# A hybrid decoder step on one core: branch 3's turned queries loaded two residues ahead, exchanged copies in a tile of their own, the weights of gb issued behind the attention, one buffer in another pool

## The chip, the cores and the metric

The kernel runs on one core of a Trainium2 chip. Its time is the device time of one execution in microseconds; the figure before the change is the median of three runs, 1337.58 us (1333.66 to 1339.45). Rows of the profile come from one further execution that was recorded by the hardware profiler.

## The reference

One inference step of a one-layer decoder with d = 1024, for a prompt of 2048 positions and a sample of 8 sequences with 8 new positions each. After an RMS norm one input projection gives the queries, keys and values (q, k, v) of mixer A, those of mixer B (qb, kb, vb), a low-rank gate input and two output gates:

```python
z = h @ w_in
q, k, v, qb, kb, vb, g_lr, gate_a, gate_b = jnp.split(z, split_points(), axis=-1)
q = rope(rmsnorm(heads(q, H_A), q_norm_w), pos)
k = rope(rmsnorm(heads(k, H_A), k_norm_w), pos)
o_a = attend(q, k, v)
log_a = jax.nn.log_sigmoid((g_lr @ w_gate_up + b_gate).astype(jnp.float32)) / GATE_TAU
o_b, s_fin = gla_chunked(heads(qb, H_B) * (DK_B ** -0.5), heads(kb, H_B), heads(vb, H_B),
                         heads(log_a, H_B), s0)
y = x + mixed.astype(x.dtype) @ w_out
```

Mixer A is a sliding-window attention with 8 heads of 64 in three branches of (window, dilation) = (128, 1), (512, 4), (2048, 16), mixed by their softmax denominators. In the third branch a position sees only positions of its own residue mod 16, so for the prompt it is 16 separate causal attentions of 128 rows each. Mixer B is a gated linear attention (GLA) with 4 heads. `mixed` is both mixers' outputs times their gates' SiLU.

## The kernel before, in words

Products are made of 16-bit halves (a value is split into a high and a low part), so one projected tile of 128 rows takes three matmuls for each of eight pieces of 128 input columns: `acc_vb` is 24 matmuls of 512 columns, `acc_g` is 24 of 272 and 24 of 256. TensorE is PE, VectorE DVE, ScalarE ACT, GpSimd POOL; SP issues all DMAs, in order.

The stages, by the trace: up to 500 us the projections q, k, v with branches 1 and 2 beside them; 500 to 623 us the projection qkb (the queries and keys of mixer B) beside the rest of the attention; 623 to 728 us branch 3; 728 to 985 us the projections g (gates) and vb with the GLA of the prompt; 985 to 1070 us the projection gb (the last gates) with the GLA of the sample; then the output projection, tile by tile, with the attention of the sample.

Branch 3 has a `branch3(r)` for each residue r (line 912), which gives two items `(r, 0)` and `(r, 1)` of four heads each to the queue `work`. A pipeline (line 1074) carries each item through three steps while the next ones follow: `qk` (scores `s` on PE at line 444, mask and maximum on DVE at 452, exponential `p` on ACT at 455), `tr` (PE turns the probabilities, `t` at 462, split into `pt` by ACT, DVE or POOL at 424 to 429) and `pv` (`O` at 477, its two parts added by ACT's `ol` at 493 and DVE's `o` at 494, stored by SP at 937). Ahead of the scores of a residue stands `pre` (line 915). It calls `turned3(r + 1)`, which lets SP load queries and keys of the next residue turned by the DMA (lines 906 to 910), and then `exchanged` (lines 815 to 818): two DVE copies of `T_q`, whose 128 partitions are two halves of 64, into the second half of the same tile with these halves swapped. Each score is a sum of two matmuls, one with the queries as loaded and one with the exchanged ones, against the keys `T_k`. `T_q` and `T_k` have two buffers each, so the load for residue r takes the buffer of r − 2 and waits for its last scores.

Beside the attention run the *host*, which deals out a projection's matmuls (`rest`, `project`), and `load_w`, which loads a projection's weights in eight pieces (line 601, tiles `wr_`), squares each on ACT for its size (line 622, `jw_`), works out a scale and splits each piece (lines 649 and 650). `weave` (line 358) mixes such parts by their share of steps done; `load_w("gb")` is a part of the second `weave` (line 1522). The sequence in which `weave` emits instructions is not the final one: a scheduler at compile time reorders each engine's program by a model of when data and buffers are ready. So a load of weights can move far ahead, as the weights of gb do: they are loaded in the middle of branch 3.

`qk_post` (line 684) makes the rotary form of q and k with two scratch tiles `t1` and `t2` from the pool `zp` (line 697); the pool `xp` closes with the projections q, k, v, before `b3`, the pool of branch 3, is opened in its place. `zp` stays open until the output stage's pools for the sample's attention take its place.

In the GLA, `gT_e`, `kq_e`, `la_e` are the first steps of a pair of chunks (e0 is the first): gate inputs and keys turned by PE and taken out by ACT, and the log of the gate in three ACT steps (lines 216 to 218); DVE scans it (223), ACT makes `eb_e` (227), then the `E` of each level (244), and PE the scores `sc_e` (281).

Of the kernel before, what the change touches and what calls it, by code (L numbers as in the profile page):

```python
# [7 lines left out]
F32 = mybir.dt.float32  # L8
F32R = mybir.dt.float32r
F16 = mybir.dt.float16  # L10
# [8 lines left out]
P = 128  # L19
# [33 lines left out]
def tile_hymba(ctx: ExitStack, tc: tile.TileContext, A: dict):  # L53
# [293 lines left out]
    def by16(ap, r):  # L347
        return ap.rearrange("(i r) c -> r i c", r=16)[r]
# [33 lines left out]
    with ExitStack() as c1:  # L382
# [206 lines left out]
        def load_w(name, between=(), behind=()):  # L589
# [7 lines left out]
            for k in range(KT):  # L597
                if k % 2 == 0:
                    pair = wr.tile([P, 2, 528], F32, name=f"wr_{name}_{k}", tag="wr")
                raw = pair[:, k % 2]  # L600
                SP.dma_start(raw[:, :n], src[k * P : (k + 1) * P, c0 : c0 + n])
                raws.append(raw)
                if k == KT // 2 - 1:
                    for f in between:
                        fetch(f)
# [78 lines left out]
        def qk_post(names, n, t):  # L684
# [9 lines left out]
                ct[:n, :, :g], cs[:n].unsqueeze(2).to_broadcast([n, 2, g, 64]),  # L694
                tabs[:n, :, i0 : i0 + g], ALU.mult,
            )
            t1 = zp.tile([P, 2, 512], F32, name=f"t1_{tag}", tag="z3", bufs=1)
            t2 = zp.tile([P, 2, 512], F32, name=f"t2_{tag}", tag="z4", bufs=1)
            z4 = zs[:n, :g].rearrange("p g (h two d) -> p g h two d", two=2, d=32)
            t24 = t2[:n, :g].rearrange("p g (h two d) -> p g h two d", two=2, d=32)  # L700
# [200 lines left out]
            return out  # L901


        T3 = [{} for _ in range(16)]

        def turned3(r):
            for nm_, src, nb in (("q", qp_d, 16), ("k", kp_d, 8)):
                t = b3.tile([P, nb, P], F16, name=f"T3_{nm_}_{r}", tag=f"T{nm_}")
                SP.dma_start_transpose(t[:, 0:8], by16(src, r))
                T3[r][nm_] = t  # L910

        def branch3(r):
            T = T3[r]

            def pre():
                if r == 0:
                    turned3(0)
                if r < 15:
                    turned3(r + 1)
                yield  # L920
                exchanged(
                    *(T["q"][:, a : a + 8].rearrange("p h i -> p (h i)") for a in (8, 0))
                )
                T["v"] = b3.tile([P, 1024], F16, name=f"v3_{r}", tag="v3")
                SP.dma_start(T["v"][:], by16(vp_d[:], r))
                for a in range(2):
                    T["o", a] = op.tile([P, 4, 66], F32, name=f"o3_{r}_{a}", tag="o")

            def OT(a, i):
                if ("O", a) not in T:  # L930
                    T["O", a] = ps_O.tile([P, 512], F32, name=f"O3_{r}_{a}", tag="O")
                return T["O", a][:, i * P : i * P + P]

            def post(a):
                o = T["o", a]
                added(o[:, :, 0:64], T["O", a][:])
                SP.dma_start(
                    by16(o3_d[:, 264 * a : 264 * a + 264], r), o[:].rearrange("p h d -> p (h d)")
                )

            return [
                attend(
                    f"3_{r}_{a}", 4, 1,
                    lambda i, a=a: [
                        (T["q"][:, 8 * part + 4 * a + i], T["k"][:, 4 * a + i])
                        for part in range(2)
                    ],
                    m3,
                    lambda i, b, a=a: T["v"][:, (4 * a + i) * P : (4 * a + i + 1) * P],
                    lambda i, a=a: T["o", a][:, i, 65:66],  # L950
                    lambda i, a=a: T["o", a][:, i, 64:65],
                    lambda i, a=a: OT(a, i),
                    pre=None if a else pre, post=lambda a=a: post(a), neg=scl["s"][:],
                )
                for a in range(2)
            ]
# [1073 lines left out]
```

## Time and profile before

| | |
|---|---|
| median of three runs | 1337.58 us |
| lowest and highest | 1333.66 and 1339.45 us |
| the profiled execution | 1341.12 us |
| its span in the profile | 1339.3 us |
| mean granted PE clock of it | 0.977 |

The profiled execution is 1.8 us longer than its span, and 1.7 us above the highest of the three. In the profile's rows, busy times are in microseconds of one engine, PEld is PE's loading of weights (beside PE's matmuls), and (x555) counts instructions. A row of waits has who waited, at which line, for what, then the total in us, how often, and the longest. A group of instructions has line, engine, operation, output and input by the program's names with buffer numbers left out, shape and count, then busy time and mean ns, then idle time ahead of them and what ended it. A row of the chain of waits has its start, its length and what it was; "issue" is time in which the engine waited for nothing that the profile shows. Rows of a timeline have start, length, engine (SPq is SP's queue of DMA issues), line and operation. A granted clock of 1.00 is PE's full speed.

### The profile page before, as it was taken

The page shows a single profiled execution, that of the slowest core. Times are in us where ns is not written, and L with a number is a line of the kernel's source. Part 1 is how long each engine was busy: PE and PEld are TensorE (multiplying, and loading weights), DVE is VectorE, ACT ScalarE, POOL GpSimd, SP SyncE. Part 2 cuts the span into 40 slices and gives each one's busy share as a digit, 9 for nine tenths or more (in the row PEclk, how much of TensorE's full clock was granted, in tenths as well). Part 3 has the DMA queues.
Part 4 walks back from the last instruction along what each step waited for, and adds up shares of the span by engine and source line. Part 5 has one row for each costly group of instructions (what it writes and reads, how often), then busy time and mean ns, then how long its engine had stood idle before and what let it go on. Part 6 is the DMA issues. An engine that isn't in the chain of part 4 may idle for free.

```text
span 1339.3 us, 26206 instructions
## 1 busy us (share of the span) xinstructions
PE 1215.7 (91%) x8878; PEld 726.8 (54%) x8878; DVE 924.8 (69%) x2275; ACT 876.6 (65%) x2332; POOL 635.4 (47%) x598
## 2 busy tenths in 40 slices
PE   3798999888899798998989899999999979999998
PEld 1343565555566555576667566676554434444443
DVE  6367767788677966776755988777682288778751
ACT  5655787777568875878986666666773366554630
POOL 0076554778678735661113975666362133232220
PEclk9998999999999999999999999999999989999999
DMA  8859856767966599969986556553236679998952
GB/s 256 248 159 254 234 174 155 208 204 216 222 180 192 174 265 281 317 208 212 214 186 184 171 179 200 163 156 119 88 126 192 193 229 342 358 380 293 320 191 79
DMA packets 251800, 285.27 MB, mean 213 GB/s; under 512 B 125441, under 2 KB 160338, under 8 KB 251666
## 3 DMA queue, kind: packets, MB, share of 16 engines
q1 hardware_dynamic: 251666, 283.60, 70.9%
q8 instruction: 70, 1.15, 0.4%
q14 instruction: 64, 0.52, 0.1%
HBM read 183.12 MB, written 75.24 MB: 193 GB/s over the span
## 4 chain that ended last, share of the span: by engine, by line
PE 38%; DVE 18%; DMA 16%; POOL 9%; issue 9%; ACT 8%; SPq 2%; POOLq 0%; DVEq 0%; ACTq 0%
PE Y L1652 4%; PE acc_qkb L1127 3%; PE acc_vb L1127 3%; PE acc_v L1127 3%; PE acc_g L1127 3%; PE acc_gb L1127 3%; PE O L477 3%; PE t L462 3%; PE s L444 3%; DVE qbd L252 3%; PE acc_q L1127 2%; DMA T_q<-qp_d 2%; POOL pr L965 2%; PE acc_k L1127 2%; DMA sv<-in_cache_v_win 2%
## 5 line engine op out<-in xcount | busy, mean ns | idle before, releaser
L1127 PEld LDWEIGHTS <-hr 128*128 128x128 f16 x1824 | 174.5, 99 | 134.3 <-issue 17.4
L1127 PEld LDWEIGHTS <-hl 128*128 128x128 f16 x1248 | 122.1, 100 | 151.8 <-issue 24.3
L455 ACT ACTIVATE p<-p,o 128x256 f32<-128x256 f32 (+1 forms) x384 | 173.3, 456 | 46.4 <-DVE o L452 39.4
L1652 PE MATMUL Y<-w_o,mh 128*128 128x512 f16 x768 | 176.7, 381 | 1.8 <-ACT mh L1611 1.8
L965 POOL TENSOR_TENSOR pr<-k,qb 128x512 f32<-128x512 f32 x96 | 132.5, 1381 | 91.2 <-DVE sck L970 57.1
L429 POOL TENSOR_TENSOR pt<-p,pt 128x512 f16<-128x512 f32 (+1 forms) x80 | 94.2, 1178 | 158.4 <-ACT pt L428 142.6
L477 PE MATMUL O<-v,pt 128*128 128x128 f16 x1200 | 111.4, 222 | 25.5 <-POOL pt L429 9.2
L1652 PEld LDWEIGHTS <-mh 128*128 128x128 f16 x768 | 72.0, 98 | 88.6 <-issue 6.3
L970 DVE TENSOR_REDUCE sck<-pr 128x8 f32<-128x512 f32 x128 | 85.6, 678 | 49.0 <-POOL pr L965 48.8
L462 PE MATMUL t<-ident,p 128*128 128x128 f32 x600 | 107.5, 284 | 8.1 <-ACT p L455 3.5
L1694 POOL TENSOR_TENSOR tc<-oc,w 128x512 f32<-128x512 f32 x32 | 45.2, 1432 | 141.9 <-DVE w L1686 119.1
L477 PEld LDWEIGHTS <-pt 128*128 128x128 f16 x1200 | 82.5, 99 | 51.2 <-POOL pt L429 14.1
L1127 PE MATMUL acc_v<-w_v,hl 128*128 128x512 f16 x384 | 96.4, 396 | 8.1 <-DMA hl<-early_ht 4.0
L1127 PE MATMUL acc_g<-w_g,hr 128*128 128x272 f16 (+1 forms) x768 | 102.6, 279 | 0.0
L452 DVE CUSTOM_DVE_ANT_0 p<-s,m3w,scl_s 128x128 f32<-128x128 f32 (+1 forms) x256 | 88.9, 394 | 11.6 <-PE s L444 6.2
L1127 PE MATMUL acc_q<-w_q,hl 128*128 128x512 f16 x384 | 91.6, 387 | 3.5 <-ACT zs_k L677 2.2
L244 ACT ACTIVATE E<-D_e 128x256 f32<-128x256 f32 x168 | 66.3, 417 | 43.5 <-POOL D_e L236 25.6
L1127 PE MATMUL acc_vb<-w_vb,hr 128*128 128x512 f16 x384 | 92.3, 389 | 2.4 <-ACT zg L733 2.4
L1127 PE MATMUL acc_k<-w_k,hl 128*128 128x512 f16 x384 | 89.9, 379 | 3.4 <-ACT zs_k L677 3.0
L444 PE MATMUL s<-kk,qq 128*128 128x256 f16 (+1 forms) x512 | 82.4, 272 | 9.7 <-DMA kk<-kp_d 6.1
L1127 PE MATMUL acc_gb<-w_gb,hr 128*128 128x512 f16 x384 | 87.1, 380 | 0.0
L462 PEld LDWEIGHTS t<-ident,p 128*128 128x128 f32 x600 | 69.4, 145 | 18.1 <-ACT p L455 8.1
(510 smaller groups left out, 2637.4 us busy)
## 6 DMA issues: line engine op xcount, KB each, us to landing
k<-in_cache_k_win SPq DMA_DIRECT2D x104, 256.0 KB
sv<-in_cache_v_win SPq DMA_DIRECT2D x24, 1024.0 KB
hr<-h_d SPq DMA_DIRECT2D x44, 512.0 KB
qb<-q_d SPq DMA_DIRECT2D x64, 256.0 KB
o_d<-o SPq DMA_DIRECT2D x96, 132.0 KB
oc<-o_d SPq DMA_DIRECT2D x48, 264.0 KB
x<-in_x_prompt SPq DMA_DIRECT2D x16, 512.0 KB
h_d<-hl SPq DMA_DIRECT2D x16, 512.0 KB
```

Source lines behind the costliest of these rows:

```text
L244: ACT.activation(ev[rows, i], dv[rows, :, half, :], AF.Exp, scale=(2 * half - 1) / 16.0)
L429: POOL.tensor_tensor(l, f, h, ALU.subtract)
L444: PE.matmul(s_ps[:, i * w : (i + 1) * w], q, k, start=(n == 0), stop=(n == len(prods) - 1),)
L452: DVE.tensor_tensor_reduce(s[:, sl], s_ps[:, sl], mask, neg, BIG, ALU.add, ALU.min, nmf(i))
L455: ACT.activation(s[:, sl], s[:, sl], AF.Exp, bias=nmf(i), scale=-1.0, accum_out=denf(i))
L462: PE.transpose(p_ps[:, i * P : (i + 1) * P], t["s"][:, i * P : (i + 1) * P], ident[:])
L477: PE.matmul(o_, t["pt"][:, c, (i * nb + b) * P : (i * nb + b + 1) * P], vf(i, b), start=(n == 0), stop=(n == 2 * nb - 1),)
L965: POOL.tensor_tensor(pr[:], kt, qt, ALU.mult)
L970: DVE.tensor_reduce(out, pr[:].rearrange("p (u k d) -> p u k d", u=2, k=4), AX.X, ALU.add)
L1127: PE.matmul(z, a_[:, k, :], w[:, p_, k, cols], start=(k == 0 and i == 0), stop=(k == KT - 1 and i == 2),)
L1652: PE.matmul(Y[:], a_[:, k, :], w_[:, part, k, :512], start=(i == 0), stop=(i == len(prods) - 1),)
L1694: eng.tensor_tensor(t_[:], oc[:, g, :, 0:64], w[:, g].unsqueeze(2).to_broadcast([P, NH, HD]), ALU.mult,)
```

## The change

Four edits:

- `turned3(r)` now loads the keys of residue r and the queries of r + 1, keys first; the queries have three buffers instead of two, so a query load takes the buffer of r − 3. One extra call, `turned3(-1)`, loads the queries of residue 0.
- The exchanged copies go to a tile `T_x` of their own; `T_q` holds 8 blocks instead of 16. The second product of each score reads `T_x`.
- The loads of the weights of gb, and only of gb, are tied by `tc.issue_after` to the last store of branch 3: SP issues them behind it.
- `t1` moves from the pool `zp` to the pool `xp`.

```diff
--- before.py
+++ after.py
@@ -598,7 +598,10 @@
                 if k % 2 == 0:
                     pair = wr.tile([P, 2, 528], F32, name=f"wr_{name}_{k}", tag="wr")
                 raw = pair[:, k % 2]
-                SP.dma_start(raw[:, :n], src[k * P : (k + 1) * P, c0 : c0 + n])
+                with ExitStack() as order:
+                    if name == "gb":
+                        order.enter_context(tc.issue_after(b3_at["SP"]))
+                    SP.dma_start(raw[:, :n], src[k * P : (k + 1) * P, c0 : c0 + n])
                 raws.append(raw)
                 if k == KT // 2 - 1:
                     for f in between:
@@ -694,7 +697,7 @@
                 ct[:n, :, :g], cs[:n].unsqueeze(2).to_broadcast([n, 2, g, 64]),
                 tabs[:n, :, i0 : i0 + g], ALU.mult,
             )
-            t1 = zp.tile([P, 2, 512], F32, name=f"t1_{tag}", tag="z3", bufs=1)
+            t1 = xp.tile([P, 2, 512], F32, name=f"t1_{tag}", tag="z3", bufs=1)
             t2 = zp.tile([P, 2, 512], F32, name=f"t2_{tag}", tag="z4", bufs=1)
             z4 = zs[:n, :g].rearrange("p g (h two d) -> p g h two d", two=2, d=32)
             t24 = t2[:n, :g].rearrange("p g (h two d) -> p g h two d", two=2, d=32)
@@ -901,26 +904,30 @@
             return out
 
 
-        T3 = [{} for _ in range(16)]
+        T3, b3_at = [{} for _ in range(16)], {}
 
         def turned3(r):
-            for nm_, src, nb in (("q", qp_d, 16), ("k", kp_d, 8)):
-                t = b3.tile([P, nb, P], F16, name=f"T3_{nm_}_{r}", tag=f"T{nm_}")
-                SP.dma_start_transpose(t[:, 0:8], by16(src, r))
-                T3[r][nm_] = t
+            for nm_, src, r_ in (("k", kp_d, r), ("q", qp_d, r + 1)):
+                if 0 <= r_ < 16:
+                    t = b3.tile(
+                        [P, 8, P], F16, name=f"T3_{nm_}_{r_}", tag=f"T{nm_}",
+                        bufs=3 if nm_ == "q" else 2,
+                    )
+                    SP.dma_start_transpose(t[:], by16(src, r_))
+                    T3[r_][nm_] = t
 
         def branch3(r):
             T = T3[r]
 
             def pre():
                 if r == 0:
+                    turned3(-1)
                     turned3(0)
                 if r < 15:
                     turned3(r + 1)
                 yield
-                exchanged(
-                    *(T["q"][:, a : a + 8].rearrange("p h i -> p (h i)") for a in (8, 0))
-                )
+                T["x"] = b3.tile([P, 8, P], F16, name=f"T3_x_{r}", tag="Tx")
+                exchanged(*(T[n_][:].rearrange("p h i -> p (h i)") for n_ in "xq"))
                 T["v"] = b3.tile([P, 1024], F16, name=f"v3_{r}", tag="v3")
                 SP.dma_start(T["v"][:], by16(vp_d[:], r))
                 for a in range(2):
@@ -934,16 +941,15 @@
             def post(a):
                 o = T["o", a]
                 added(o[:, :, 0:64], T["O", a][:])
-                SP.dma_start(
+                b3_at["SP"] = SP.dma_start(
                     by16(o3_d[:, 264 * a : 264 * a + 264], r), o[:].rearrange("p h d -> p (h d)")
-                )
+                ).ins
 
             return [
                 attend(
                     f"3_{r}_{a}", 4, 1,
                     lambda i, a=a: [
-                        (T["q"][:, 8 * part + 4 * a + i], T["k"][:, 4 * a + i])
-                        for part in range(2)
+                        (T[n_][:, 4 * a + i], T["k"][:, 4 * a + i]) for n_ in "qx"
                     ],
                     m3,
                     lambda i, b, a=a: T["v"][:, (4 * a + i) * P : (4 * a + i + 1) * P],
```

What it does to SP's program, in the middle of branch 3. Names: `T3_q_9` and `T3_k_9` are the turned queries and keys of residue 9, `o3_3_1` is the output of item (3, 1) (its store comes some three items after the scores), `v3_6` the values of residue 6, `wr_gb_0` the first two pieces of the weights of gb. Before:

```order
L601 DMA wr_gb_0_9553<-in_w_in 128x512 x2
L909 DMA_TRANSPOSE T3_q_8_8479<-qp_d_74 128x8x128
L909 DMA_TRANSPOSE T3_k_8_8481<-kp_d_73 128x8x128
L601 DMA wr_gb_2_9556<-in_w_in 128x512 x2
L937 DMA o3_d_69<-o3_3_1_7999 128x264
L601 DMA wr_gb_4_9559<-in_w_in 128x512 x2
L601 DMA wr_gb_6_9562<-in_w_in 128x512 x2
L937 DMA o3_d_69<-o3_4_0_8120 128x264
L925 DMA v3_6_8372<-vp_d_75 128x1024
L909 DMA_TRANSPOSE T3_q_9_8588<-qp_d_74 128x8x128
L909 DMA_TRANSPOSE T3_k_9_8590<-kp_d_73 128x8x128
```

The same stretch after:

```order
L932 DMA v3_5_8263<-vp_d_75 128x1024
L916 DMA_TRANSPOSE T3_q_9_8490<-qp_d_74 128x8x128
L916 DMA_TRANSPOSE T3_k_8_8488<-kp_d_73 128x8x128
L944 DMA o3_d_69<-o3_3_1_8005 128x264
L932 DMA v3_6_8381<-vp_d_75 128x1024
L737 DMA zg_d_62<-zg0_0_9592 128x16
L738 DMA ga_d_65<-zg0_0_9592 128x256
L944 DMA o3_d_69<-o3_4_0_8127 128x264
L916 DMA_TRANSPOSE T3_k_9_8598<-kp_d_73 128x8x128
L916 DMA_TRANSPOSE T3_q_10_8600<-qp_d_74 128x8x128
L944 DMA o3_d_69<-o3_4_1_8128 128x264
```

The eight loads of weights are gone from here, and the queries of a residue go out with the keys of the residue before: `T3_q_9` stood behind `o3_4_0` with `T3_k_9` and stands ahead of `o3_3_1` now, and behind `o3_4_0` now stand `T3_k_9` and `T3_q_10`. In DVE's program the two copies of a residue keep their place, behind the mask of the second item two residues back (those of residue 10 behind the mask of (8, 1)).

SP's program at the end of branch 3, after the change; before, `scan_m` stood right behind the store of `o3_15_1`:

```order
L944 DMA o3_d_69<-o3_15_1_9284 128x264
L604 DMA wr_gb_0_9569<-in_w_in 128x512 x2
L604 DMA wr_gb_2_9572<-in_w_in 128x512 x2
L604 DMA wr_gb_4_9575<-in_w_in 128x512 x2
L604 DMA wr_gb_6_9578<-in_w_in 128x512 x2
L1244 DMA scan_m_9454<-in_c_scan 128x256
L1246 DMA gmask_9453<-in_c_gmask 64x7x32 x2
L987 DMA qb_6_0_9972<-q_d_58 128x512
```

The eight loads stand behind the last store now, ahead of the GLA's tables (`scan_m`, `gmask`) and the sample's `qb` and `k`.

ACT's program at the end of branch 3 and the beginning of the GLA. `ol_352` belongs to the last output of branch 3; `vbs_3`, `zg0_4` and `zg1_4` take tiles 3 and 4 of the host's projections out of PSUM; `jw_gb_0` is the square of the first piece of weights. Before (the three steps of `la_e0`, `gT_e1`, `eb_e0`, `vbs_4` and the first `E0` follow):

```order
L493 ACTIVATE ol_347_9378<-O3_14_1_9369 128x256
L493 ACTIVATE ol_350_9400<-O3_15_0_9391 128x256
L746 ACTIVATE vbs_3_9965<-acc_vb_3_9924,wi_vb_8191 128x512
L493 ACTIVATE ol_352_9413<-O3_15_1_9404 128x256
L199 ACTIVATE kq_e0_9866<-ptg_e0_0_9873 128x2x128
L202 ACTIVATE kq_e0_9866<-ptg_e0_0_9873 128x2x128
L733 ACTIVATE zg0_4_10021<-acc_g0_4_9970,wi_g_6631 128x272
L191 ACTIVATE gT_e0_9867<-pg_e0_9869 16x256
L199 ACTIVATE kq_e0_9866<-ptg_e0_1_9880 128x2x128
L202 ACTIVATE kq_e0_9866<-ptg_e0_1_9880 128x2x128
L738 ACTIVATE zg1_4_10080<-acc_g1_4_10025,wi_g_6631 128x256
L216 ACTIVATE la_e0_9905<-u_e0_9902 128x512
```

After (the same steps follow, with `jw_gb_4` to `jw_gb_7` among them):

```order
L493 ACTIVATE ol_352_9429<-O3_15_1_9420 128x256
L199 ACTIVATE kq_e0_9882<-ptg_e0_0_9889 128x2x128
L202 ACTIVATE kq_e0_9882<-ptg_e0_0_9889 128x2x128
L191 ACTIVATE gT_e0_9883<-pg_e0_9885 16x256
L625 ACTIVATE jw_gb_0_9581,wm_gb_9568<-wr_gb_0_9569,nw_81 128x512
L625 ACTIVATE jw_gb_1_9667,wm_gb_9568<-wr_gb_0_9569,nw_81 128x512
L749 ACTIVATE vbs_3_9981<-acc_vb_3_9940,wi_vb_8198 128x512
L625 ACTIVATE jw_gb_2_9753,wm_gb_9568<-wr_gb_2_9572,nw_81 128x512
L199 ACTIVATE kq_e0_9882<-ptg_e0_1_9896 128x2x128
L202 ACTIVATE kq_e0_9882<-ptg_e0_1_9896 128x2x128
L216 ACTIVATE la_e0_9921<-u_e0_9918 128x512
L625 ACTIVATE jw_gb_3_9839,wm_gb_9568<-wr_gb_2_9572,nw_81 128x512
```

The host is less far when the attention ends (`vbs_3` stood ahead of `ol_352` and stands behind it), and the eight squares, which stood in the middle of branch 3, stand among the first steps of the GLA. Before, 67 matmuls of `acc_g` and 24 of `acc_vb` stood in PE's program between the last output of branch 3 and the first `sc_e`; now 53 and 47 do. From there to the output stage PE's program is as before. In the output stage, where the pools of the sample's attention take the place of `zp`, loads and first steps of the sample are ordered differently: PE turns `ls_q` and `ls_k` (line 1781) ahead of the first tile's `tm` (line 1610) instead of behind it, and SP issues `ls_k` behind three loads of `oc` (line 1669).

## The prediction, made before the run

> **What bounds the kernel now.** I read the page first, then the work by stretches, the list of waits, the groups of instructions, and last the chain of waits where those pointed. The page says which engine is full over the whole run:
>
> ```profile
> PE 1215.7 (91%) x8878; PEld 726.8 (54%) x8878; DVE 924.8 (69%) x2275; ACT 876.6 (65%) x2332; POOL 635.4 (47%) x598
> ```
>
> PE is busy for 91% of the span, so little can be won except where PE stands. The change touches branch 3 of the attention (622.8 to 728.3 us) and what follows it. The stretches compare that stage with the one just before, in which the projection qkb runs beside the attention (after the two times: length, busy time of each engine, granted PE clock, DMA share, GB/s):
>
> ```profile
> 560.00:622.80 62.80, 62.80 (x555) 44.96 (x554) 43.64 (x159) 51.62 (x169) 30.13 (x25) 1.00 0.79 221
> 622.80:728.30 105.50, 93.75 (x867) 72.92 (x866) 65.60 (x282) 87.89 (x318) 18.17 (x17) 0.94 0.81 191
> ```
>
> Before the stage PE is full at clock 1.00. In the stage it idles 105.5 − 93.75 = 11.75 us, its clock is 0.94, and ACT idles 105.5 − 87.89 = 17.6 us. No engine is full; so a latency bounds it. Which, the waits say (what waited, for what, total us, times, longest; the first row is of all engines from 480 to 720, the others of PE from 590 to 745):
>
> ```profile
> DVE T_q L818 <- DMA T_q<-qp_d: 26.6, 11, 3.4
> ...
> PE s L444 <- DVE o L452: 5.2, 3, 3.3
> PE O L477 <- DVE o L494: 2.9, 3, 2.2
> PE t L462 <- DVE pt L425: 2.6, 1, 2.6
> ```
>
> DVE waits for the turned queries, and PE waits 5.2 + 2.9 + 2.6 = 10.7 of its 11.75 us for DVE. The groups of the stage (busy us, mean ns; behind the second bar the idle time before them and what ended it) say the same for ACT:
>
> ```profile
> L455 ACT ACTIVATE p<-p,o 128x128 f32<-128x128 f32 x102 | 39.8, 398 | 4.6 <-DVE o L452 4.5
> ...
> L493 ACT ACTIVATE ol<-O 128x256 f32<-128x256 f32 x28 | 10.6, 377 | 8.6 <-DVE o L494 5.2 <-PE O L477 3.3
> L818 DVE COPY T_q<-T_q 64x1024 f16<-64x1024 f16 x22 | 10.1, 459 | 20.4 <-DMA T_q<-qp_d 20.1
> L622 ACT ACTIVATE jw_gb<-wr_gb,nw 128x512 bf16<-128x512 f32 x8 | 5.7, 713 | 0.0
> L746 ACT ACTIVATE vbs<-acc_vb,wi_vb 128x512 f32<-128x512 f32 x4 | 2.7, 678 | 0.6 <-PE acc_vb L1127 0.6
> L622 ACT ACTIVATION_READ_ACCUMULATOR jw_gb<-wr_gb,nw 128x1 f32 x8 | 1.5, 193 | 0.0
> ```
>
> Of ACT's 17.6 idle us, 4.5 + 5.2 = 9.7 end with a DVE instruction, and DVE stood 20.1 us before its copies. The chain of waits shows one round of it (start, us, what):
>
> ```profile
> 659.28 0.61 PE O L477 x8
> ...
> 660.11 0.22 PE s L444 x4
> ...
> 660.64 4.81 DMA T_q<-qp_d
> ...
> 665.48 0.42 DVE T_q L818
> ...
> 665.91 0.43 DVE T_q L818
> ...
> 666.36 0.44 DVE o L494
> ...
> 666.84 0.39 PE O L477 x5
> 667.23 5.46 DMA T_q<-qp_d
> ```
>
> The scores of an item free the query buffer, the next transpose goes out and takes 4.8 to 5.5 us, and the copies, which stand in DVE's program right behind the mask of that same item, hold the output (o) and the next mask behind them. The wait is not needed by the copies' reader, which is an item away; it costs because DVE runs in order.
>
> **The change part by part: branch 3.** The copies keep their place in DVE's order, but by the order of SP the queries they read now go out after the scores of the item before: one residue earlier. With the stage at 105.5 us a residue lasts 105.5 / 16 = 6.6 us, and at the 88.7 us worked out below 5.5 us. The query transfer goes out behind the key transfer of its pair; of such a pair the first takes SP 1.26 us and the second 1.96 (the last two rows are for the weights, below):
>
> ```profile
> 660.64 1.26 SPq L909 DMA_TRANSPOSE T_q<-qp_d  x1
> ...
> 662.83 1.96 SPq L909 DMA_TRANSPOSE T_k<-kp_d  x1
> ...
> 641.36 0.82 SPq L601 DMA_DIRECT2D wr_gb<-in_w_in  x2
> ...
> 729.25 0.43 SPq L1238 DMA_DIRECT2D scan_m<-in_c_scan  x1
> ```
>
> So it lands 1.3 + 5.2 = 6.5 us after those scores, up to 7.2 with the second's longer issue, and the copy comes a residue after them plus the mask, at about 6: a wait of some 1 us may be left, but the steps of ACT and PE that it holds are now a residue of work away instead of next. I take DVE's share of ACT's idle time as gone.
>
> What the stage then lasts, from three sides. PE: 93.75 us of which 0.06 × 93.75 = 5.6 us is lost to the clock, so 88.1 us at full clock; less the 6.6 us that move out (next part) leaves 81.5 us, if PE is full as it was from 560 to 622.8. ACT: 87.89 us, less the eight squares of the gb weights (5.7 + 1.5 us, of which some overlaps, so 8 × 0.8 = 6.4) and one vbs (0.7) that move out, is 80.8 us; with the 17.6 − 9.7 = 7.9 us of idle time that DVE did not cause it is 88.7 us. Or ACT as full as from 560 to 622.8, 51.62 / 62.80 = 0.82, which gives 80.8 / 0.82 = 98.5 us. I take 88.7 us, since the idle time in it is that of this very stage: a gain of 16.8 us, with ends of 24.0 and 7.0. DMA does not bind: 0.81 × 105.5 = 85.5 us, less 2 MB of weights at the rate of this row (8.5 us), is 77 us:
>
> ```profile
> 620.00:630.00 10.00, 6.82 (x87) 6.33 (x85) 6.66 (x33) 7.19 (x27) 1.16 (x1) 0.98 1.09 246
> ```
>
> **Projection work that moves out.** The host (the projections g and vb, dealt out between the attention's steps) is further behind when the attention ends: by the order 23 matmuls of acc_vb and 14 of acc_g fewer stand ahead of the last output of branch 3. The chain prices them:
>
> ```profile
> 709.30 1.74 PE acc_g L1127 x15
> ...
> 718.71 2.37 PE acc_vb L1127 x11
> ```
>
> 23 × 2.37 / 11 + 14 × 1.74 / 15 = 5.0 + 1.6 = **6.6 us**, which PE does later, where it has almost no idle time to hide them in (+6.6):
>
> ```profile
> 800.00:900.00 100.00, 95.87 (x860) 66.94 (x859) 77.86 (x121) 63.46 (x172) 61.63 (x51) 0.98 0.57 179
> ```
>
> **Weights of gb behind the attention.** The eight loads were issued near 641 us; now the first goes out behind the last output store, at 729.25 where scan_m stood, 0.41 us apart (0.82 / 2). When they land, two loads of the same size in the chain bound, and a transfer under heavy load:
>
> ```profile
> 463.38 3.56 DMA wr_g<-in_w_in
> ...
> 541.86 5.89 DMA wr_vb<-in_w_in
> ...
> 1102.29 10.77 DMA Sc<-sc_d
> ```
>
> I take 4.7 us, between the first two: 733.9, and the others 256 KB / 246 GB/s = 1.07 us apart. Their squares stand in ACT's program in between the gate chain of e0 (|u|, exp, ln at lines 216 to 218), and ACT waits in order for them:
>
> ```profile
> 727.98 0.38 ACT L493 ACTIVATE ol<-O 128x256 f32<-128x256 f32 x1 [1.38 <-PE O L477]
> ...
> 729.53 0.36 ACT L191 ACTIVATE gT_e<-pg_e 16x256 f32<-16x256 f32 x1
> ...
> 733.25 0.60 ACT L216 ACTIVATE la_e<-u_e 128x512 f32<-128x512 f32 x1 [0.58 <-PE u_e L210]
> ...
> 734.54 0.72 ACT L218 ACTIVATE la_e<-la_e,ones 128x512 f32<-128x512 f32 x1
> ...
> 739.35 2.46 ACT L244 ACTIVATE E<-D_e 128x256 f32<-128x256 f32 x6
> ```
>
> Walking the order: squares 0 and 1 end at 734.7 and 735.5, vbs 736.1, square 2 736.9, the kq pair 737.5, |u| 738.1, square 3, exp 739.5, square 4, ln 741.0, against 735.3 before; the scans on DVE and eb follow, and the first E starts at 745.1 instead of 739.35, **5.8 us later**. PE has 3.3 us more host work ahead of the first scores of e0 than it had there, which covers that much: it stalls 5.8 − 3.3 = **2.5 us**. Ends: 0 if the loads land in 3.56 us and the host finds other work, and about 9 if they take the 10.77 us of the last row. The Trainium skill ("DMA: Bandwidth & Descriptors", section "Anatomy of one DMA", measured there for transfers issued from GpSimd) puts a transfer at about 2.0 us plus its bytes over 436 GB/s; an estimate by it is 2.6 us to land and 0.6 us apart, E at about 743.1, a stall of 0.5 us and a sum of −9.2 instead of −7.2. The transfers above, at 3.56 and more, do not bear that out; the sum goes by them.
>
> **Output stage.** The buffer moved to another pool rearranges the last 270 us: in the new order PE turns the sample's ls_q and ls_k before the first tile's tm, not behind it, and SP issues ls_k behind three oc transfers that wait for a buffer.
>
> ```profile
> 1092.30 1.04 PE L1610 MATMUL tm<-ident,mt 128*128 128x128 f16 x8 [8.86 <-ACT mt L1600]
> ...
> 1087.38 0.79 SPq L1669 DMA_DIRECT2D oc<-o_d  x2
> ...
> 1092.51 0.60 SPq L1778 DMA_DIRECT2D ls_k<-k_d  x1
> ```
>
> PE idles 8.86 us there already. If ls_k lands after mt is ready, PE waits for it instead, up to about another 8 us; if earlier, nothing is lost. The earlier loads of the sample could also gain a little at 1102 (10.77 us, above). I take +0.5, ends −3 and +8.
>
> The third query buffer and the separate tile for the copies are space, not time; the number of transposes is 32 as before, the extra early one costs SP 1.26 us beside a full PE, and elsewhere the order is the same.
>
> Sum: −16.8 + 6.6 + 2.5 + 0.5 = **−7.2 us**. The profiled execution took 1341.1 us (span 1339.3), above the highest of the three timed runs; the difference is what I carry over: 1341.1 − 7.2 = 1333.9 there, and 1337.6 − 7.2 = 1330.4 for the median.
>
> **The rivals.** *PE becomes the bound*: the stage shrinks to 81.5 us, 7.2 less than forecast; −14.4, 1323.2 us. For it: PE was full in the stage before with the same kind of mixture, ACT at 0.82 there. Against: ACT would have to be 99% busy (80.8 of 81.5).
>
> *ACT's chain becomes the bound*: at ACT's 0.82 the stage lasts 98.5 us; +9.8 on the forecast, so +2.6, 1340.2 us. For it: softmax steps wait for PE as well (3.3 us of ol), and a late copy still holds DVE when a residue falls under 6.5 us.
>
> *Slower, by the keys*: T_k keeps two buffers and goes out where it did, after the scores of (r−2, 1). They were always covered by the copies' wait for T_q; uncovered, PE's scores wait for T_k itself, and the stage stays at 105.5 us. Then only the costs remain: 6.6 + 2.5 + 0.5 = +9.6, 1347.2 us. It decides if the keys land later than 1.5 residues after that, 1.5 × 5.5 = 8.3 us; with 5.5 us in flight that needs 2.8 us of queueing on SP. Against: the transposes go out first in their pair now and the gb loads, 3.3 us of SP's time, have left the stage; and PE has no wait for T_k in the rows above.
>
> That the change doesn't lead the queries at all is ruled out by SP's order.
>
> **How the numbers follow.** 0.5% is 6.7 us, about what a measurement of this kernel can tell from no change. The forecast has 0.50, with a range of its own of 1326 to 1335 us; its middle is 0.5 us past the bound, so 0.27 of it counts as faster and 0.23 as same. PE as the bound 0.20, faster; ACT's chain 0.15, same; the keys 0.15, slower. Faster 0.47, same 0.38, slower 0.15. The range reaches from 1321 (PE's bound with 2 us of the output stage's gain) to 1341 (ACT's chain), leaving out the keys and a little below.
>
> **What would show it.** Right: in branch 3 the wait of DVE's copies for T_q falls from 20 us to under 5, the stage lasts about 89 us with PE's clock near 1.00, the first E of e0 stands about 16 us after the last ol instead of 11.4, and PE waits there 2 to 3 us. Wrong: a wait of PE for T_k (keys); a stage of 98 us with ACT's waits on PE (ACT's chain); PE idle by more than 5 us before the first scores of e0, or by more than 12 us before the first tm of the output stage.

## The result and the profile after

| | before | after |
|---|---|---|
| median | 1337.58 us (17 runs, 1333.66 to 1341.45) | 1346.92 us (17 runs, 1339.61 to 1353.05) |
| ratio, with its 95% interval | 1 | 1.0068 [1.0054, 1.0082] |
| span of the profiled execution | 1339.3 us | 1345.7 us |

The change made the kernel slower by 0.68%, 9.1 us [7.2, 11.0]; 7.2 us faster was forecast. PE's busy time is nearly the same (1215.7 us before), and the span is longer:

```profile
PE 1219.1 (91%) x8878; PEld 728.4 (54%) x8878; DVE 932.6 (69%) x2275; ACT 878.4 (65%) x2332; POOL 633.7 (47%) x598
```

The two traces are laid beside each other at points that both have: the end of the last `acc_qkb`, the last `ol` of branch 3, the first and last `acc_gb`, the first and last `Y` (from the timelines of PE and ACT; us).

| stretch | before | after | difference |
|---|---|---|---|
| start to the end of qkb | 618.3 | 616.5 | −1.8 |
| qkb to the last `ol` | 110.1 | 101.9 | −8.2 |
| last `ol` to the first `acc_gb` | 226.2 | 236.9 | +10.7 |
| `acc_gb` | 128.9 | 127.4 | −1.5 |
| last `acc_gb` to the first `Y` | 11.1 | 16.1 | +5.0 |
| first `Y` to the end | 244.9 | 246.9 | +2.0 |

Branch 3 is shorter by 8.2 us, but the GLA behind it is longer by 10.7; and the output stage loses 7.0 us (5.0 + 2.0). First branch 3 of the kernel after, as a stretch:

```profile
620.30:718.40 98.10, 86.51 (x835) 68.94 (x833) 70.01 (x280) 81.91 (x301) 18.59 (x17) 0.95 0.79 181
```

PE idles 98.1 − 86.5 = 11.6 us here, as before (11.75). What became shorter is its work: it is the host's matmuls that left (37, of `acc_vb` and `acc_g`, by the order). Two rows of DVE's list of waits before (590 to 728 us):

```profile
DVE o L494 <- ACT ol L493: 10.5, 8, 3.8
...
DVE p L452 <- DMA o_d<-o: 0.6, 2, 0.4
```

And in the kernel after (590 to 718 us):

```profile
DVE p L452 <- DMA o_d<-o: 10.4, 7, 3.4
DVE o L494 <- ACT ol L493: 9.9, 11, 3.0
DVE p L452 <- PE t L462: 5.1, 3, 3.2
```

The wait for T_q, 26.6 us in the list of before, is gone as forecast. In its place the mask (line 452) waits 10.4 us for stores of o to land. The mask also writes its maximum into the item's output tile o; seven such tiles go round, and the eighth item needs one whose store has been read out. PE's own list and the groups of that stage:

```profile
PE s L444 <- DMA T_k<-kp_d: 3.8, 1, 3.8
PE t L462 <- ACT p L455: 2.6, 1, 2.6
PE s L444 <- DVE o L452: 2.4, 2, 1.8
```

```profile
L455 ACT ACTIVATE p<-p,o 128x128 f32<-128x128 f32 x102 | 39.8, 396 | 8.8 <-DVE o L452 8.8
...
L452 DVE CUSTOM_DVE_ANT_0 p<-s,m3w,scl_s 128x128 f32<-128x128 f32 x100 | 29.4, 346 | 16.2 <-DMA o_d<-o 10.4 <-PE t L462 5.1 <-issue 0.6
...
L821 DVE COPY T_x<-T_q 64x1024 f16<-64x1024 f16 x22 | 13.7, 624 | 1.1 <-PE s L444 0.6
```

The copies wait 1.1 us where they waited 20.4, but ACT's exponential now waits 8.8 us for the mask, where it waited 4.6. The chain of waits of the kernel after shows the new round (a row of `o_d<-o` runs from the issue of a store to its landing):

```profile
661.15 3.88 DMA o_d<-o
...
665.19 0.35 DVE p L452
...
669.23 2.27 DMA o_d<-o
...
671.66 0.35 DVE p L452
...
672.33 5.30 DMA o_d<-o
...
677.79 0.35 DVE p L452
```

So a store takes 2.27 to 5.30 us from its issue here. Some stores are also issued late: SP's timeline has them behind transposes in its queue. The last one below goes out at 677.52 us, and its o was complete at 674.2 us. What share of the 10.4 us comes from late issue is not shown.

```profile
659.80 1.25 SPq L916 DMA_TRANSPOSE T_q<-qp_d  x1
661.15 1.75 SPq L944 DMA_DIRECT2D o_d<-o  x1
...
672.80 1.43 SPq L916 DMA_TRANSPOSE T_k<-kp_d  x1
674.28 3.14 SPq L916 DMA_TRANSPOSE T_q<-qp_d  x1
677.52 0.53 SPq L944 DMA_DIRECT2D o_d<-o  x1
```

At the beginning of the GLA, the loads of the weights in SP's timeline, and then ACT's:

```profile
719.82 3.77 SPq L604 DMA_DIRECT2D wr_gb<-in_w_in  x8
```

```profile
718.01 0.38 ACT L493 ACTIVATE ol<-O 128x256 f32<-128x256 f32 x1 [0.19 <-PE O L477]
...
722.69 0.72 ACT L625 ACTIVATE jw_gb<-wr_gb,nw 128x512 bf16<-128x512 f32 x1 [3.52 <-DMA wr_gb<-in_w_in]
...
732.87 2.45 ACT L244 ACTIVATE E<-D_e 128x256 f32<-128x256 f32 x6
```

ACT stands 3.5 us for the weights, and the first `E` comes 14.9 us behind the start of the last `ol`, against 11.4. PE does not idle while ACT stands (from 718 to 735 us it is busy for all of the 17.00 us), since it has the host's left-over work.

The GLA's stretch, from the end of the last `ol` to the first `acc_gb`, before and then after:

```profile
728.40:954.50 226.10, 214.97 (x1895) 148.32 (x1892) 183.70 (x273) 144.42 (x385) 154.22 (x129) 0.98 0.53 164
```

```profile
718.40:955.30 236.90, 224.72 (x1935) 153.55 (x1933) 183.79 (x274) 151.04 (x403) 152.69 (x129) 0.97 0.54 168
```

So of the 10.7 us PE is busy for 9.8, and idle for only 1 us more. The moved matmuls are 6.6 us of that by the prediction's prices. PE's granted clock is also lower at the beginning, up to 800 us: 0.94 after (0.94 and 0.93 in e4 and e5 below, which have the same program there) against 0.98 before. What lowers it is not shown.

In the output stage, PE's timeline:

```profile
1090.45 0.69 PE L1787 MATMUL ts_q<-ident,ls_q 64*128 64x64 f32 x4 [7.73 <-DMA ls_q<-q_d]
...
1094.52 0.66 PE L1787 MATMUL ts_k<-ident,ls_k 64*128 64x64 f32 x4 [2.76 <-DMA ls_k<-k_d]
...
1096.01 1.06 PE L1616 MATMUL tm<-ident,mt 128*128 128x128 f16 x8
...
1098.83 1.04 PE L1658 MATMUL Y<-w_o,mh 128*128 128x512 f16 x4
```

PE waits 7.7 + 2.8 us for the sample's loads where it waited 8.9 for `mt`, and the first `Y` comes 16.1 us behind the last `acc_gb` instead of 11.1.

### The profile page after: what moved, and what is told of

Same layout as the page of the kernel before. It is cut to its first block, busy times and chain, and to the rows that moved or that the text cites. A ratio compares the mean times of both kernels' runs of the same rounds, so it can differ in the third digit from the quotient of the medians.

```text
span 1345.7 us, 26205 instructions
## 1 busy us (share of the span) xinstructions
PE 1219.1 (91%) x8878; PEld 728.4 (54%) x8878; DVE 932.6 (69%) x2275; ACT 878.4 (65%) x2332; POOL 633.7 (47%) x598
## 4 chain that ended last, share of the span: by engine, by line
PE 33%; DVE 19%; DMA 16%; issue 11%; ACT 9%; POOL 8%; SPq 2%; POOLq 0%; DVEq 0%; ACTq 0%
DVE qbd L252 3%; PE Y L1658 3%; PE acc_qkb L1133 3%; PE acc_vb L1133 3%; PE t L462 3%; PE acc_g L1133 3%; PE s L444 3%; PE O L477 2%; PE acc_gb L1133 2%; PE acc_q L1133 2%; DVE p L452 2%; POOL pr L971 2%; PE acc_v L1133 2%; DMA o_d<-o 2%; PE acc_k L1133 2%
## 5 line engine op out<-in xcount | busy, mean ns | idle before, releaser
L452 DVE CUSTOM_DVE_ANT_0 p<-s,m3w,scl_s 128x128 f32<-128x128 f32 (+1 forms) x256 | 89.2, 395 | 28.8 <-DMA o_d<-o 10.4
L444 PE MATMUL s<-kk,qq 128*128 128x256 f16 (+1 forms) x512 | 82.2, 272 | 10.2 <-DMA kk<-kp_d 6.5
```

The costliest lines, as they stand in the source:

```text
L444: PE.matmul(s_ps[:, i * w : (i + 1) * w], q, k, start=(n == 0), stop=(n == len(prods) - 1),)
L452: DVE.tensor_tensor_reduce(s[:, sl], s_ps[:, sl], mask, neg, BIG, ALU.add, ALU.min, nmf(i))
```

## The experiments

Theory 1: what costs is t1's place (it lengthens the output stage) and the tie, that is, holding the gb loads behind the attention. Theory 2, formed after e3: the leading of the queries, that is, loading them a residue earlier, gives nothing because the o tiles bound branch 3 next. Each expectation names its own rival; that the keys bind, a rival of the prediction, is among them. Each kernel was run 7 to 12 times, in turn with the kernel before (median 1336.9 to 1338.3 us in these).

| kernel | against before: us [95% interval] | qkb to first acc_gb | last acc_gb to first Y |
|---|---|---|---|
| before | 0 | 336.3 | 11.1 |
| after | +9.1 [7.2, 11.0] | 338.8 | 16.1 |
| e1: t1 in xp alone | +4.3 [2.1, 6.6] | 334.8 | 15.8 |
| e2: gb tie alone | +5.9 [2.7, 9.0] | 337.7 | 9.6 |
| e3: after without the tie | +5.5 [3.2, 7.8] | 335.1 | 16.4 |
| e4: after, sample turned behind tm | +6.6 [3.7, 9.5] | 336.1 | 15.4 |
| e5: after, sample turned behind Y | +9.2 [6.4, 11.9] | 338.5 | 14.3 |
| e6: e3 with nine o tiles | +0.9 [−1.7, 3.7] | 328.6 | 16.1 |
| e7: after, tie at residue 9 | +7.1 [4.3, 9.9] | 332.0 | 16.6 |
| e8: e6, sample turned behind Y | −2.4 [−5.1, 0.3] | 329.2 | 14.6 |
| e9: queries and copies alone | −0.3 [−2.8, 2.3] | 336.3 | 9.8 |
| **e10: e9 with nine o tiles** | **−5.0 [−7.9, −2.1]** | 329.6 | 10.3 |
| e11: e1 with nine o tiles | +2.9 [0.8, 5.2] | 334.2 | 16.3 |
| e12: after with nine o tiles | +7.5 [4.1, 10.7] | 333.2 | 16.8 |
| e13: e12, squares behind eb | +6.6 [3.5, 9.8] | 326.7 | 15.2 |
| e14: e10, tie at residue 9 | +2.1 [−0.3, 4.7] | 337.0 | 9.9 |

The second column is the ratio of the timed runs less 1, times 1337.6 us; the last two are read from one profiled execution each, so a difference of 2 us between two kernels there says little (e1 has the program of before up to the output stage, and differs by 1.5). The profiled execution of before, 1341.1 us, is itself one of its longest.

**e1**, t1 alone:

```diff
-            t1 = zp.tile([P, 2, 512], F32, name=f"t1_{tag}", tag="z3", bufs=1)
+            t1 = xp.tile([P, 2, 512], F32, name=f"t1_{tag}", tag="z3", bufs=1)
```

> Only t1 is moved from zp to xp; up to the output stage the order of all engines is that of before. Theory 1 (the output stage pays): in the changed kernel PE stood 7.7 + 2.8 us for ls_q and ls_k, where before it stood 8.9 us for mt, and its output stage ended 5.5 to 6 us later from the same start (acc_gb ends at 1080.2 and 1080.4). So this kernel is slower than before by 4 to 7 us, with PE's wait for ls_q in its profile. Rival (the later end comes from loads that branch 3's edits shift, and a buffer's place costs nothing): within 1.5 us of before.

It was 4.3 us slower, in the stretch ahead of the first `Y`. Theory 1 holds here: the place of one scratch tile, not a load shifted by branch 3, makes the output stage longer.

**e2**, the tie alone:

```diff
+                with ExitStack() as order:
+                    if name == "gb":
+                        order.enter_context(tc.issue_after(b3_at["SP"]))
+                    SP.dma_start(raw[:, :n], src[k * P : (k + 1) * P, c0 : c0 + n])
```

> Only the loads of the gb weights are tied behind the last store of branch 3; queries, copies and t1 as before. Theory 1 (the moved host work and squares are given back behind branch 3): the stage of branch 3 ends earlier by 5 to 10 us since 30 matmuls and 8 squares leave it, the first E stands 4 to 6 us further behind the last ol than the 11.4 us of before, and PE's granted clock dips there; at 798 us of before the kernel is late by 2 to 5 us, and the whole is slower by 2 to 5 us. Rival (the loads out of branch 3 relieve SP and DMA there, and this pays): faster by 2 us or more. Rival (keys): no difference to theory 1 here.

It was 5.9 us slower. From the end of qkb to the last `ol` it took 99.9 us (before 110.1), the first `E` came 4.1 us later than before behind it, and PE idled 25.9 us from the end of qkb to the first `acc_gb` instead of 22.9. PE's clock did not dip there (0.98 up to 800 us), so that part of theory 1 was wrong. Branch 3 is as much shorter here as in the kernel after (101.9), though the queries are not led: the shorter stage comes from the work that left it. Its profiled execution (1339.2 us) was among the shortest of its runs, so the trace shows less than the whole loss.

**e3**, the kernel after without those four lines:

> The changed kernel with the loads of the gb weights free again (they go out in the middle of branch 3); queries two ahead, copies apart and t1 in xp stay. Theory 1: branch 3's gain is real but was spent behind it, so here 3 to 7 us of it remain against the 5.5 us that the output stage costs: between 2.5 us faster and 2.5 us slower than before. Rival (keys: PE's wait for T_k, 3.8 us in one piece in the changed kernel, and DVE's wait for the stores of o, 10.4 us, take the whole of the gain): branch 3 lasts as long as before and the kernel is slower by the 5 to 6 us of the output stage, as e1.

It was 5.5 us slower, as e1 and above the range of theory 1. Against e1 the leading of the queries gave nothing that the times show, and in the list of waits DVE's mask waited 16.3 us for stores of o, which the rival had named beside the keys. From here on theory 2 was tested.

**e4** and **e5**, the kernel after with PE's order of before in the output stage; e4 queues `sample_new` behind the last `tm` of the first tile, e5 behind its first `Y` (the lines are e5's):

```diff
         def sample_attention():
-            sample_new()
+            with tc.issue_after(y_at["PE"]):
+                sample_new()
```

> The changed kernel with PE's turning of ls_q and ls_k queued behind the first tile's last tm, as it stood before; all else unchanged. Theory 1 (PE's order is what costs in the output stage): PE waits for mt again, not for ls_q, and 4 to 6 us of the 9.3 us loss come back: 3 to 5 us slower than before. Rival (the loads of the sample that SP now issues ahead delay the tile's own oc, zl and obl loads, so mt itself is later): less than 2 us come back, and the wait for mt is 12 us or more instead of 8.9.

> The changed kernel with PE's turning of ls_q and ls_k queued behind the first matmuls of the first tile's Y, where it stood before. In e4 it stood between tm and Y, and PE's first Y still came 5.7 us behind the first tm instead of 2.2. Theory 1 (PE's order costs): the stretch from the last acc_gb to the end falls from 263 us to 255 to 258 (before: 255.9), and the kernel is 3 to 5 us slower than before instead of 9.1. Rival (the sample's loads, which SP now issues ahead of the tile's own, delay the first tile): no better than e4, 6 us or more slower than before.

e4 was 2.5 us faster than the kernel after, inside the noise of the two, and e5 no faster; that PE's order alone costs falls. In e5 the timelines of PE, POOL and DVE show why:

```profile
1095.43 1.03 PE L1616 MATMUL tm<-ident,mt 128*128 128x128 f16 x8 [2.79 <-ACT mt L1606]
1099.63 1.03 PE L1616 MATMUL tm<-ident,mt 128*128 128x128 f16 x8 [3.17 <-DVE mt L1607]
```

```profile
1091.49 0.40 POOL L1810 COPY Scg<-Sc 128x256 f32<-128x256 f32 x1 [1.50 <-DMA Sc<-sc_d]
1091.85 1.71 POOL L1708 TENSOR_TENSOR tc<-tc,tc 128x512 f32<-128x512 f32 x1
```

```profile
1096.85 0.19 DVE L1686 TENSOR_REDUCE mn<-oc 128x8 f32<-128x24 f32 x1 [2.57 <-DMA oc<-o_d]
...
1098.35 1.22 DVE L1607 TENSOR_TENSOR mt<-mix,mt 128x1024 f16<-128x1024 f32 x1
```

POOL's sum for the first tile stands behind a copy of the sample's `Sc`, which waits for its load, and DVE's second half of `mt` stands behind a step of the third tile that waits 2.6 us for `oc`. The first half of `tm` starts 9.3 us behind the last `acc_gb` (8.9 before) and the second half 13.5 us (10.2 before), so in e5 the loss is for the most part DVE's. In the kernel after PE's own order holds the first tile as well; putting one of the three engines right leaves the others.

**e6**, e3 with two more o tiles:

```diff
-        op = c_att.enter_context(tc.tile_pool(name="op", bufs=7))
+        op = c_att.enter_context(tc.tile_pool(name="op", bufs=9))
```

> e3 (queries two ahead, copies apart, t1 in xp, gb loads free) with nine instead of seven buffers for the output tile o. In e3 DVE's mask waited 16.3 us for stores of o (o_d), where before its copies waited 23 us for T_q. Theory 2 (the wait for a free o tile took the place of the wait for the queries): that wait falls under 4 us, branch 3 falls from 107.7 to 98 to 103 us, and 4 to 8 us come back: from 2.5 us faster to 1.5 us slower than before, where e3 was 5.5 slower. Rival (the pipeline is bound by its own round through PE, DVE and ACT, and idle time only changes its name): DVE's wait for o_d goes, but branch 3 stays at 105 us or more and the kernel within 2 us of e3.

It was 0.9 us slower, 4.6 us better than e3; from the end of qkb to the last `ol` it took 101.0 us with 930 matmuls, where e3 took 107.7 with 933, and the mask no longer waited for stores of o. PE still waited 2.7 us for keys. Theory 2 holds.

**e7**, the kernel after with the tie at the stores of residue 9:

```diff
-                b3_at["SP"] = SP.dma_start(
+                st_ = SP.dma_start(
...
+                if r == 9:
+                    b3_at["SP"] = st_
```

> The changed kernel with the gb loads tied behind the stores of residue 9 instead of the last one: they leave the middle of branch 3 but land before its end. Theory 1 (their late landing holds ACT at the first steps of the GLA, where PE idles and its clock dips): ACT's wait for wr_gb goes (3.5 us in one piece), PE's clock from the end of branch 3 to 800 us is 0.97 or more instead of 0.94, and 3 to 5 us come back: 4 to 6 us slower than before. Rival (what costs is that the host is behind by some 30 matmuls whenever the loads leave the middle): within 1.5 us of the changed kernel, 8 to 10 us slower than before.

It was 7.1 us slower, between the two expectations, and its interval holds most of both. The first `E` came 11.1 us behind the end of the last `ol`, as before, so ACT's stand was gone, and PE's clock up to 800 us was 0.98; little time came back with them.

**e8**, e6 with e5's edit:

> e6 (gb loads free, nine o tiles) with the turning of ls_q and ls_k behind the first Y as in e5. If both theories hold, the costs of the output stage and of the o tiles are gone and the leading of the queries pays: 3 to 8 us faster than before. If only theory 1 holds: within 2.5 us of before. If neither: 4 us slower or more.

At −2.4 us it lies at the edge between the first two of its cases, and its interval reaches just over zero; it decides nothing.

**e9**, the leading of the queries and the separate copies alone. The space that the change found by moving t1 is found elsewhere: the exchanged copies lie in tiles of the queries of branches 1 and 2, which are free by then.

```diff
-                T["x"] = b3.tile([P, 8, P], F16, name=f"T3_x_{r}", tag="Tx")
+                x_ = ap_.tile([P, 2, 4, 512], F16, name=f"T3_x_{r}", tag="qq")
+                T["x"] = x_[:, 0, 0:2].rearrange("p a (b i) -> p (a b) i", i=P)
```

> Only the queries two ahead and the copies apart: the exchanged copies lie in the query tiles of branches 1 and 2 (tag qq, free by then), so t1 can stay in zp; gb loads free, seven o tiles. Theory 1 and 2 together: the output stage is that of before again (254 to 256 us from the last acc_gb to the end, against 260 to 263), and the wait for o tiles still takes the gain of branch 3: within 2.5 us of before, with DVE waiting 10 us or more for stores of o. Rival (the leading itself costs, by the keys): 4 us slower or more, with PE waiting for T_k.

**e10**, the same with nine o tiles:

> e9 with nine tiles for o. Theory 2 (o tiles are what the leading of the queries runs into) with theory 1 (the place of t1 and the tie of gb are the costs): from the last acc_qkb to the first acc_gb 328 to 331 us instead of before's 335 to 336, the output stage as before, so 4 to 8 us faster than before. Rival (e8's and e6's gain came from elsewhere, the chip's noise among it): within 2.5 us of before.

e9 took the same time as before, and e10 was 5.0 us faster: both as theory 2 has it, and e10 beats both kernels. The mask's group of branch 3, in e9 and then in e10:

```profile
L452 DVE CUSTOM_DVE_ANT_0 p<-s,m3w,scl_s 128x128 f32<-128x128 f32 x112 | 32.7, 346 | 17.3 <-DMA o_d<-o 11.7 <-PE t L462 5.3 <-PE s L444 0.2
```

```profile
L452 DVE CUSTOM_DVE_ANT_0 p<-s,m3w,scl_s 128x128 f32<-128x128 f32 x112 | 32.8, 345 | 5.3 <-PE t L462 2.8 <-POOL pt L429 1.2 <-PE s L444 0.7
```

With nine tiles the 11.7 us for stores of o are gone. The stretches of branch 3, e9 and e10:

```profile
618.60:727.80 109.20, 99.25 (x962) 79.31 (x960) 76.71 (x313) 96.43 (x351) 19.94 (x19) 0.95 0.85 210
```

```profile
615.60:717.20 101.60, 96.03 (x967) 76.56 (x965) 73.64 (x313) 95.39 (x351) 19.81 (x19) 0.98 0.93 225
```

For about the same work the stage is 7.6 us shorter: PE's idle time falls from 10.0 to 5.6 us, its busy time by 3.2 us at a granted clock of 0.98 instead of 0.95, and ACT is busy for 94% of the stage. The size is that of two single executions, and e10's was the shortest of its twelve (1328.2 us, median 1333.0). The direction is borne out by the other kernels whose gb loads are free: with the queries led and nine tiles the stage took 101.0 to 103.4 us (e6, e8, e10), with seven tiles 107.7 and 109.2 (e3, e9).

**e11**, e1 with nine o tiles, queries as before:

> e1 (before with t1 in xp) with nine tiles for o; queries as before. Theory 2: before, DVE's copies wait for T_q and its masks hardly for stores of o (0.6 us), so more o tiles alone give nothing: within 2 us of e1, 3 to 7 us slower than before. Rival (o tiles are worth 5 us by themselves, and leading the queries nothing): within 2.5 us of before.

It was 2.9 us slower, within 2 us of e1, and its copies still waited for the queries:

```profile
DVE T_q L818 <- DMA T_q<-qp_d: 19.0, 8, 3.4
```

Its stage took 108.2 us. So neither the tiles nor the leading pays alone.

**e12**, the kernel after with nine o tiles:

> The changed kernel, its gb tie too, with nine tiles for o; beside e6 it differs by the tie alone. Theory 1 (the tie costs behind the attention): 3 to 6 us slower than e6, so 4 to 7 us slower than before, with ACT's wait for wr_gb of 3 us or more at the first steps of the GLA. Rival (the tie only cost since branch 3 was held up by o tiles): within 1.5 us of e6.

It was 7.5 us slower, 6.6 us worse than e6, which differs by the tie alone. That the tie cost only because of the o tiles falls. With seven tiles it cost 5.9 us alone (e2) and 3.6 us in the changed kernel (after against e3); these prices do not differ beyond their noise. DVE's waits for the gate's logarithm from the end of branch 3 to 800 us, e12 and then e6:

```profile
DVE la_e L219 <- ACT la_e L218: 6.0, 2, 3.3
```

```profile
DVE la_e L219 <- ACT la_e L218: 0.7, 1, 0.7
```

**e13**, e12 with the squares queued behind `eb` of e0:

```diff
+                        if name == "gb":
+                            order.enter_context(tc.issue_after(eb_at["e0"]))
                         ACT.activation(
                             jk[:, :n], raws[k][:, :n], AF.Square, scale=rows[:, k : k + 1],
```

> e12 (the changed kernel with nine o tiles) with the eight squares of the gb weights queued behind eb of e0 on ACT; loads tied as before, the host's lag unchanged. Theory 1 (the tie costs since squares and their loads stand ahead of the gate's logarithm, DVE waits 6 us for la and the GLA's first steps come late): the stretch from the last ol to the first E falls from 15.0 to 11 to 12 us, DVE's wait for la under 3 us, and 3 to 6 us come back: 1.5 to 4.5 us slower than before instead of 7.5, near e6. Rival (the tie costs since the host is some 45 matmuls behind when branch 3 ends): the first E comes earlier, but the time stays within 2 us of e12.

The trace went theory 1's way in part (13.7 us to the first `E`, a wait of 2.7 us for la, 6.5 us less up to the first `acc_gb`), but that execution was among the shortest of its kernel; over all runs it was 6.6 us slower than before, within 1 us of e12, as the rival had it.

**e14**, e10 with the tie of e7:

> e10 (queries two ahead, nine o tiles, t1 in zp) with the gb loads tied behind the stores of residue 9. Theory 1 (a tie costs only where the squares meet the GLA's first steps): within 2 us of e10, 3 to 7 us faster than before. Rival (the tie costs by the host's lag or by gb's later split wherever the loads go): 3 us or more slower than e10, so no faster than 2 us against before.

It was 7 us slower than e10, as the rival had it, though nothing of gb met the GLA's first steps. In branch 3 PE idled 12.4 us, where e10 had 5.6, and the copies waited for the queries again:

```profile
DVE T_x L821 <- DMA T_q<-qp_d: 8.5, 3, 4.1
```

In e10 that wait was 2.2 us. So the tie costs inside branch 3 as well, and theory 1 is not enough for it. Why is open: the loads in the way are not the whole of it, since 9.7 of PE's 12.4 idle us fall before the first load of gb goes out at 682.3 us.

## Why the prediction was wrong

**The wait for the queries.** The step "I take DVE's share of ACT's idle time as gone" failed. The cause before was read rightly, and the wait for T_q did go. But the stage was held by a second round just behind the first: mask, o, store, landing, free o tile. In the profile of before it showed as 0.6 us in a list, since a DVE that waits for the queries asks for o tiles late enough. I asked what is late next of PE and ACT and of the keys, and did not count the tiles: an item holds one of the seven o tiles from its mask to the landing of its store, so a mask waits for the store of seven items before. e9 is the measure of the step: no gain (−0.3 [−2.8, 2.3] us) where the sum has a stage 16.8 us shorter, 10.2 us with the moved work taken off. e10 shows what it is worth when the next limit is moved too, 5.0 [2.1, 7.9] us.

**The moved work.** That branch 3 would end earlier and the host's work come back behind it was right in kind: the stage lost 37 matmuls and 8.2 us, and 10.7 us came back. The 8.2 us are little more than the work that left (6.6 us), e2 has them without the led queries, and the GLA behind took more than that back.

**The tie.** The first `E` was forecast 5.8 us later and came 3.5 us later (first weight 722.7 − 719.8 = 2.9 us after its issue, less than the 4.7 taken; of the two loads behind that figure wr_g has 528 columns, not 512). The stall of 2.5 us ahead of `sc_e` did not show: PE was full there. PE idled elsewhere instead, 3 us more from the end of qkb to the first `acc_gb` in e2 (25.9) than before (22.9) and in e12 (21.5) than in e6 (18.5): in e2 behind the first `E`, in e12 half of it in branch 3. By the runs the tie costs 5.9 [2.7, 9.0] us (e2). If the moved work cancels (less in branch 3, more behind it), that is inside the ends of 0 and 9 us that I gave the stall, but not by the stall. What of it is the squares' place and what the host's lag or branch 3 itself is not settled: e7, e13 and e14 speak against the squares alone.

**The output stage.** Taken at +0.5, it cost 4.3 [2.1, 6.6] us in e1, and 7.0 us in the traces: the ends of −3 and +8 held it, the value was wrong. I weighed one engine's wait ("if earlier, nothing is lost") where the new order put waits ahead of the first tile on PE, POOL and DVE together (e5).

**The rivals.** The rival on the slower side, the keys, gave 1347.2 us and 1346.9 was measured, but that is luck, since its mechanism is not what the runs show. PE's scores did wait for keys, 3.8 us in one piece; in e9 they waited 2.2 us and the time was that of before, and with nine o tiles the keys, loaded as in e9, allowed a stage 7.6 us shorter. The terms that it took over were wrong too: an output stage of 0.5 us and a stage of 105.5. The rival of ACT's chain gave a stage of 98.5 us with ACT 0.82 busy, and 98.1 us with 81.9 / 98.1 = 0.83 was measured; that is luck too, since ACT's exponential waited 8.8 us for DVE's mask and not for PE. PE was not the bound: it idled 11.6 us. e10, with ACT at 94%, comes nearest to a stage bound by ACT.

The three edits alone give −0.3 + 5.9 + 4.3 = 9.9 us, and together 9.1 [7.2, 11.0]: they add up within their noise (e9's copies lie in other tiles than those of the kernel after).

The estimate by the Trainium skill ("DMA: Bandwidth & Descriptors", section "Anatomy of one DMA"), 2.6 us to land for 256 KB, is nearer to the 2.9 us between the first issue and its square here than my 4.7, though the page measured transfers issued from GpSimd; it changed the sum by 2 us and not its sign.

## What to carry to other kernels

When a wait on an in-order engine is to be removed, count every ring of buffers (tiles that are used in turn) that the engine's next instruction takes part in, from first write to the landing of its last store; the next limit may show as half a microsecond in the profile of before, and then both must move together (e9: 0, e10: −5.0 us). Where a scheduler orders the program, a scratch tile moved to make room is an edit of its own: look at what the new order puts ahead of the first work of the next stage on all engines, not on the fullest one. And a stage that ends earlier because work left it has gained nothing yet.

## What the runs showed that was not expected

The copies of the queries took 459 ns each within one tile before and 624 ns into a tile of their own (523 in e10), 64 x 1024 of 16 bits each time. The place of a scratch tile of 4 KB a partition that only the projections of q and k use moved the beginning of the last stage by 5 us. And the spread of single executions, 1333.7 to 1341.5 us before and 1339.6 to 1353.1 after, is as large as the effect. e2, e10, e11 and e13 were each profiled in their shortest or second shortest execution. e2, e11 and e13 are slower than before by their medians, but the traces alone would have made them faster.
